# A list-scheduled two-layer decoder kernel: another order of pieces, chunks and groups, and one output store on another queue

## The chip, the cores and the metric

One core of a Trainium2 chip runs the kernel. The metric is the device time of one execution in microseconds. The kernel has one launch, and everything that it needs comes from DRAM.

## The reference

Two layers over 256 tokens of width 1024. Each layer norms x, projects it to 3584 columns that belong to three head groups, runs three kinds of attention, gates each with silu, and adds the output projection to x. A final norm follows.

```python
for layer in range(2):
    h = rms_norm(x, norm_g[layer])
    proj = einsum('btd,dc->btc', h, w_in[layer])
    sb_q, sb_k, sb_v, sb_g, mb_q, mb_k, mb_v, mb_g, mem_q, mem_g = split(proj)
    o_sb = stick_breaking(sb_q, sb_k, sb_v) * silu(sb_g)              # 6 heads of 64
    o_mb = causal softmax of rotary(mb_q), rotary(mb_k), mb_v * silu(mb_g)  # 6 heads
    m = rms_norm(mem, mem_norm_g[layer])
    mk, mv = split(einsum('bmd,dc->bmc', m, w_mem_kv[layer]))
    o_mem = softmax attention(mem_q, mk, mv) * silu(mem_g)            # 4 heads
    x = x + einsum('btc,cd->btd', concat(o_sb, o_mb, o_mem), w_out[layer])
return rms_norm(x, final_norm_g)
```

Stick-breaking weights are a sigmoid times a running product of (1 - sigmoid), worked out in log space with a cumulative sum. With 256 tokens MoBA has one block, so it is plain causal softmax.

## The kernel before

**Weights.** All weights, 81,920 words in each of 128 partitions, stream through SBUF once. They come in *pieces* (`sb_qk`, `mb_k`, `mk`, `wo0` and so on, one for each group of output columns) cut into *chunks* of some k-rows (k is one of eight blocks of 128 input rows; `NKP` says how many go into a chunk). SyncE (SP) issues a chunk's load into the ring `raw`. ScalarE (ACT) casts it to fp32r into the ring `hl` (line 287, the "hi" half), VectorE (DVE) subtracts the cast from the original (line 293, the "lo" half). TensorE (PE) then forms hi times hi, hi times lo and lo times hi. For a piece in the table `DBL` a 512-column and a 256-column matmul do this, else three 256-column ones. `HLC` is the size of the `hl` ring; the `raw` ring gets `17664 - 2 * HLC` words, so the two trade places.

**Inputs.** x comes in transposed blocks `uT`. ACT and DVE scale each by the norm's gain and split it into `T` (lines 289, 297). The row norm itself comes later: `rcx` holds it for x and `rcm` for the memory; DVE transposes it to `rt`, and it travels over DRAM to become the broadcast `rbx` or `rbm`, with which `sb_q`, `sb_k`, `mem_q` and `mem_k` are multiplied on DVE.

**Turns.** Some values have to be transposed between token and head layout. DVE transposes blocks of 32 by 32 into a buffer `D` (lines 875, 984), SP stores it to a DRAM buffer `Z` (line 1003, 128x768 words), and four or more loads bring it back turned (line 1016) to `F`, `T`, `uT` or `ga`. For a name in the table `HALVES` each of the four loads is cut into two.

**Half-array matmuls.** Scores and weighted sums of heads of 64 use 64 rows (`64*128`) or 64 columns (`128*64`) of the PE array; projections use all (`128*128`).

**Order.** Each instruction's place on its engine is fixed when the kernel is built. A list scheduler in Python holds generators (tasks) for the parts and, step by step, issues the one that can start first by planned times, broken by priorities. Its inputs are tables at the top: the order of pieces (`ORDER`), chunk sizes (`NKP`), whether a piece runs k-major (`KMAJ`), the groups of heads whose scores and weighted sums run together (`SCG`, `PVG`), priorities (`PRI`, `P_*`), the chunks behind which input blocks, x rows and constants are loaded (`X_AT`, `X0_AT`, `CST_AT`) and planned costs (`DVE_W`, `DVE_HI`, `SLACK`). On the chip each engine runs its list in order and waits on semaphores for the others.

**The end.** `out_task` ends the final norm of each of two row tiles: ACT scales columns 640 to 1023, DVE the others in two instructions, and each of the three is stored from the queue of the engine that the tuple names.

Of the kernel before, what the change touches and what calls it, by code (L numbers as in the profile page):

```python
# [41 lines left out]
PRI = ({"sb": (-170, -370), "mb": (-66, -22), "mem": (-112, 4)}, {"sb": (544, -132), "mb": (-550, -56),
       "mem": (-154, 774)})
P_EV = -3
P_H0 = -966
P_RX = -76
P_M0 = 194
P_RM = -253
P_M1 = 58
# [19 lines left out]
P_SILU = 848
SCG = (((("sb", 2), ("sb", 1)), (("sb", 0), ("mem", 1), ("mem", 0)), (("mb", 0), ("mb", 1), ("mb", 2))),  # L70
       ((("mb", 0), ("sb", 1), ("sb", 0)), (("mem", 0), ("mb", 2)), (("mb", 1),), (("sb", 2),), (("mem", 1),)))
PVG = (((("mem", 1), ("sb", 1), ("mem", 0)), (("sb", 2), ("mb", 2), ("mb", 0), ("mb", 1)), (("sb", 0),)),
       ((("mb", 0),), (("sb", 0), ("mem", 1), ("mb", 1), ("mem", 0)), (("sb", 1), ("sb", 2)), (("mb", 2),)))
# [8 lines left out]
AHEAD = 4
DVE_HI = 11539.2
SLACK_PE = 70.0
SLACK = 50.0
# [148 lines left out]
def hybrid_trunk(ctx: ExitStack, tc: tile.TileContext, x, mem, norm_g, w_in, w_mem_kv, w_out,  # L234
                 final_norm_g, xT, memT, gcols, consts, out):
    nc = tc.nc
# [762 lines left out]
    def trip(D, F, e, name, need=(), alloc=()):  # L999

        _, (Z,) = yield R("sp", alloc=["Z"])
        Zv = Z[:, :4 * e]
        nc.sync.dma_start(Zv, D[:, :4 * e])
# [8 lines left out]
        Fv = F[:, :4 * e].rearrange("p (i e) -> p i e", i=4)
        for j in range(4):
            for i0 in range(0, 4, 2 if name in HALVES else 4):
                i1 = i0 + (2 if name in HALVES else 4)
                nc.sync.dma_start(Fv[32 * j:32 * j + 32, i0:i1],
                                  Zv.rearrange("(i r) (j e) -> j r i e", i=4, j=4)[j, :, i0:i1])
# [346 lines left out]
```

## Time and profile before

| | |
|---|---|
| median of 3 runs | 268.99 us (268.93 to 269.72) |
| profiled execution, its span | 269.36 us, 267.6 us |
| PE busy | 257.0 us, 96% of the span, 1613 matmuls |
| DVE busy | 227.1 us, 85% |
| ACT busy | 193.0 us, 72% |
| SP's transfers | 77.2% of 16 DMA engines' time, 67.07 MB in all |
| granted PE clock | 0.993 of full |

The profile is of one execution. A row that groups instructions reads: line, engine, operation, output from input, shapes, count, then busy time in us and the mean of one in ns, then idle time of the engine just ahead of them and what ended it. A row of a timeline reads: start in us, duration, engine, line, operation, and in brackets the idle time before it with its releaser. `SPq` and `ACTq` rows are the engines' issuing of transfers.

### The profile page before, as it was taken

The page shows a single profiled execution, that of the slowest core. Times are in us where ns is not written, and L with a number is a line of the kernel's source. Part 1 is how long each engine was busy: PE and PEld are TensorE (multiplying, and loading weights), DVE is VectorE, ACT ScalarE, POOL GpSimd, SP SyncE. Part 2 cuts the span into 40 slices and gives each one's busy share as a digit, 9 for nine tenths or more (in the row PEclk, how much of TensorE's full clock was granted, in tenths as well). Part 3 has the DMA queues.
Part 4 walks back from the last instruction along what each step waited for, and adds up shares of the span by engine and source line. Part 5 has one row for each costly group of instructions (what it writes and reads, how often), then busy time and mean ns, then how long its engine had stood idle before and what let it go on. Part 6 is the DMA issues. An engine that isn't in the chain of part 4 may idle for free.

```text
span 267.6 us, 4996 instructions
## 1 busy us (share of the span) xinstructions
PE 257.0 (96%) x1613; PEld 228.9 (86%) x1613; DVE 227.1 (85%) x555; ACT 193.0 (72%) x429; POOL 6.2 (2%) x18
## 2 busy tenths in 40 slices
PE   8999999898999999999999999999999999999990
PEld 5878999798999997877888999888988998877880
DVE  4786988999899998999999578579999999698462
ACT  4768998689996987886876445558677988983132
POOL 1000120200000000000000000000000000000000
PEclk9999999999999999999999999999999999999997
DMA  6989999889999888997985678788597499993004
GB/s 206 367 273 342 351 393 336 289 245 277 296 305 261 263 260 284 324 299 228 299 267 178 195 182 264 221 258 275 172 283 249 162 308 282 286 281 106 0 4 157
DMA packets 50378, 67.07 MB, mean 251 GB/s; under 512 B 4720, under 2 KB 41968, under 8 KB 50352
## 3 DMA queue, kind: packets, MB, share of 16 engines
q1 hardware_dynamic: 49264, 64.65, 77.2%
q0 software_dynamic: 512, 1.31, 1.6%
q10 hardware_dynamic: 576, 0.79, 0.9%
q8 instruction: 13, 0.21, 0.3%
q14 instruction: 13, 0.11, 0.1%
HBM read 57.29 MB, written 9.44 MB: 249 GB/s over the span
## 4 chain that ended last, share of the span: by engine, by line
PE 72%; DVE 5%; DMA 5%; ACT 2%; issue 1%; ACTq 0%; DVEq 0%; SPq 0%
PE bank L270 71%; DMA gb<-in_mem_dram 3%; DMA raw<-in_w_mem_kv_dram 2%; DVE hl L293 2%; ACT junk L289 1%; DVE a L808 1%; PE bank L276 1%; DVE bank L293 1%; DVE xs L293 0%; ACT hl L287 0%; DVE gT L293 0%; DVE T L297 0%; DVE sb_k L297 0%; DVE xs L301 0%; DVE w L293 0%
## 5 line engine op out<-in xcount | busy, mean ns | idle before, releaser
L293 DVE TENSOR_TENSOR hl<-raw,hl 128x384 fp32r<-128x384 f32 (+5 forms) x146 | 103.9, 731 | 4.9 <-ACT hl L287 4.0
L270 PE MATMUL bank<-T,hl 128*128 128x256 f32 (+1 forms) x646 | 105.0, 322 | 0.7 <-DVE T L297 0.6
L287 ACT CAST hl<-raw 128x384 fp32r<-128x384 f32 (+5 forms) x144 | 91.5, 663 | 16.9 <-DMA raw<-in_w_in_dram 5.9
L270 PEld LDWEIGHTS bank<-T,hl 128*128 128x128 f32 x646 | 92.6, 189 | 11.4 <-DVE T L297 0.8
L270 PE MATMUL bank<-hl,T 128*128 128x384 f32 (+2 forms) x464 | 80.4, 330 | 0.0
L270 PEld LDWEIGHTS bank<-hl,T 128*128 128x128 f32 x464 | 77.5, 188 | 1.8 <-issue 0.7
L270 PE MATMUL bank<-hl,mxhi 128*128 128x512 f32 (+1 forms) x144 | 41.5, 369 | 0.0
L270 PEld LDWEIGHTS bank<-hl,mxhi 128*128 128x128 f32 x144 | 26.0, 188 | 5.3 <-DVE mxlo L293 0.4
L270 PE MATMUL bank<-hl,mxlo 128*128 128x512 f32 (+1 forms) x72 | 26.4, 366 | 0.0
L875 DVE STREAM_TRANSPOSE D<-w 128x384 f32<-128x384 f32 (+1 forms) x32 | 18.7, 594 | 1.0 <-ACT w L289 0.9
L289 ACT ACTIVATE junk<-xs 128x512 bf16<-128x512 f32 (+1 forms) x12 | 7.4, 613 | 16.2 <-DVE xs L293 14.7
L270 PEld LDWEIGHTS bank<-hl,mxlo 128*128 128x128 f32 x72 | 13.6, 188 | 2.2
L289 ACT ACTIVATE T<-uT,gc 128x256 fp32r<-128x256 f32 x24 | 11.6, 509 | 5.2 <-DMA uT<-xT_dram 5.0
L289 ACT ACTIVATE a<-bank 128x384 f32<-128x384 f32 x24 | 11.4, 486 | 3.7 <-DVE bank L293 2.8
L808 DVE TENSOR_TENSOR_SCAN a<-a,a 128x256 f32<-128x256 f32 (+1 forms) x24 | 12.8, 537 | 0.7 <-ACT a L289 0.7
L297 DVE SCALAR_TENSOR_TENSOR T<-uT,gc,T 128x256 fp32r<-128x256 f32 x24 | 11.3, 480 | 2.0 <-ACT T L289 1.9
L289 ACT ACTIVATE w<-w,st 128x128 f32<-128x128 f32 (+1 forms) x24 | 10.6, 444 | 0.9 <-DVE st L828 0.9
L289 ACT ACTIVATE a<-a 128x384 f32<-128x384 f32 x24 | 11.1, 520 | 0.1
L301 DVE TENSOR_SCALAR w<-w,st 128x256 f32<-128x256 f32 (+1 forms) x40 | 11.0, 323 | 0.0
L293 DVE TENSOR_TENSOR xs<-bank,xs 128x512 f32<-128x512 f32 (+1 forms) x8 | 5.3, 657 | 5.3 <-PE bank L270 5.3
L289 ACT ACTIVATE w<-bank,st 128x256 f32<-128x256 f32 x16 | 7.5, 484 | 2.1 <-DVE st L841 2.1
L828 DVE CUSTOM_DVE_ANT_0 w<-bank,cmask 128x128 f32<-128x128 f32 (+1 forms) x24 | 7.4, 347 | 1.0 <-PE bank L270 0.8
(109 smaller groups left out, 213.2 us busy)
## 6 DMA issues: line engine op xcount, KB each, us to landing
raw<-in_w_in_dram SPq DMA_DIRECT2D x28, 384.0 KB, 4.9
raw<-in_w_in_dram SPq DMA_DIRECT2D x50, 192.0 KB, 4.5
Z<-D SPq DMA_DIRECT2D x16, 384.0 KB, 4.8
raw<-in_w_out_dram SPq DMA_DIRECT2D x24, 256.0 KB, 5.5
raw<-in_w_in_dram SPq DMA_DIRECT2D x8, 576.0 KB, 5.4
raw<-in_w_mem_kv_dram SPq DMA_DIRECT2D x6, 384.0 KB, 4.5
F<-Z SPq DMA_DIRECT2D x24, 96.0 KB, 5.3
T<-Z SPq DMA_DIRECT2D x24, 96.0 KB, 4.4
```

Of the source, the lines that this page charges most:

```text
L270: nc.tensor.matmul(out, lhsT=lhsT, rhs=rhs, start=start, stop=stop, **kw)
L276: nc.tensor.transpose(out, in_, idt)
L287: nc.scalar.copy(out, in_)
L289: nc.scalar.activation(out, in_, func, **kw)
L293: nc.vector.tensor_tensor(out, a, b, op=op)
L297: nc.vector.scalar_tensor_tensor(out, a, s, b, op0=op0, op1=op1)
L301: nc.vector.tensor_scalar(out, a, s, None, op0=op)
L808: nc.vector.tensor_tensor_scan(a[:, r0:r1], a[:, r0:r1], u[:, r0:r1], 0.0, OP.add, OP.add)
L828: nc.vector.tensor_tensor_reduce(w[:, r0:r1], sc[:, r0:r1], cmask[:, 256 - r1 + r0:256], -1.0, 3.0e38, OP.add, OP.min, st[:, t:t + 1])
L875: nc.vector.transpose(o, w[:, :n * 128].rearrange("p (m j r) -> p m j r", j=4, r=32))
```

## The change

It gives new values to most tables, so the scheduler plans another order and cuts the weights into fewer, larger chunks. `HLC` goes from 6656 to 6144 words, so the `raw` ring from 4352 to 5376. Three more edits: the planned ready times of turns get 300 ns more and those of the loads of x and the memory 200 ns (in the plan only); every transfer, also one that is not issued by SP, now counts in the planner's list of transfers under way (`ring`); and the first row tile's store of columns 640 to 1023 is issued by SP instead of ACT. The names' line numbers grow by 2 or 3.

```diff
 COLS = {...}
-HLC = 6656
+HLC = 6144
 RAWC = 17664 - 2 * HLC
...
-X_AT = {7: 4, 8: 5, 11: 6, 13: 7}
-CST_AT = 34
-X0_AT = 21
+X_AT = {5: 4, 6: 5, 9: 6, 10: 7}
+CST_AT = 14
+X0_AT = 9
 X1_AT = 13
...
+ML_W = 0.0
+ML_T = 300.0
+ML_S = 200.0
 MEM_AT = 0
-ORDER = (["sb_qk", "mem_q", "mb_q", "mb_k", "mb_g", "sb_v", "mb_v", "mk", "mv", "sb_g", "mem_g"], ["mk", "mv",
-         "mb_q", "mb_k", "sb_k", "mem_q", "mb_v", "sb_q", "mem_g", "sb_v", "mb_g", "sb_g"])
+ORDER = (["sb_qk", "mb_k", "mem_q", "mb_q", "mk", "mb_v", "mv", "sb_v", "sb_g", "mb_g", "mem_g"], ["mk",
+         "mb_k", "mb_q", "mem_q", "sb_q", "sb_k", "mv", "mb_v", "mem_g", "mb_g", "sb_v", "sb_g"])
...
-HOLD = 30000.0
-HALVES = []
+HOLD = 800.0
+HALVES = [("F", 1, "sb", 2), ("F", 1, "mb", 0)]
...
 DBL = (("sb_qk", 0), ("sb_q", 1), ("sb_k", 1), ("sb_g", 1), ("mb_g", 1), ("mem_q", 0), ("mem_q", 1), ("mem_g",
-       0), ("mem_g", 1), ("mk", 1), ("mv", 1))
-DVE_W = -19195.9
+       0), ("mem_g", 1), ("mk", 1), ("mv", 0), ("mv", 1))
+DVE_W = -36995.9
...
         t = queue(_free(dst) * 4 * dst.shape[0], dst.shape[-1] * 4, now)
-        if q is None:
-            ring.append(t)
+        ring.append(t)
         if name:
-            S.ready[name] = t
+            S.ready[name] = t + {"raw": ML_W, "x": ML_S, "mem": ML_S}.get(name[0], 0.0)
...
         S.res["Z"].items.append((t, None, Z))
-        S.ready[name] = t
+        S.ready[name] = t + ML_T
         return F
...
-        for eng, a, b, q in (("act", 640, D, nc.scalar), ("dve", 0, 256, nc.sync), ("dve", 256, 640, nc.sync)):
+        for eng, a, b, q in (("act", 640, D, nc.scalar if t else nc.sync), ("dve", 0, 256, nc.sync), ("dve", 256, 640, nc.sync)):
```

The chunks change on DVE as follows: 146 subtractions (16 of 256 words, 52 of 384, 28 of 512, 34 of 768, 8 of 1024, 8 of 1152) become 107 (20 of 384, 18 of 512, 41 of 768, 14 of 1024, 6 of 1152, 8 of 1536).

First, SP's queue near the start of the program, before:

```order
L375 DMA raw<-in_w_in_dram 128x768
L375 DMA uT<-xT_dram 128x256
L375 DMA raw<-in_w_in_dram 128x768 x3
L375 DMA uT<-xT_dram 128x256
L375 DMA raw<-in_w_in_dram 128x768
L375 DMA uT<-xT_dram 128x256
L375 DMA raw<-in_w_in_dram 128x768
L375 DMA raw<-in_w_in_dram 128x256 x2
L375 DMA uT<-xT_dram 128x256
L375 DMA raw<-in_w_in_dram 128x256 x2
L375 DMA uT<-xT_dram 128x256
L375 DMA xs<-in_x_dram 128x1024
```

and now:

```order
L378 DMA raw<-in_w_in_dram 128x768
L378 DMA uT<-xT_dram 128x256
L378 DMA raw<-in_w_in_dram 128x768
L378 DMA uT<-xT_dram 128x256
L378 DMA raw<-in_w_in_dram 128x768
L378 DMA uT<-xT_dram 128x256
L378 DMA raw<-in_w_in_dram 128x768 x3
L378 DMA uT<-xT_dram 128x256
L378 DMA xs<-in_x_dram 128x1024
L378 DMA raw<-in_w_in_dram 128x384
L378 DMA uT<-xT_dram 128x256
L378 DMA raw<-in_w_in_dram 128x384 x3
```

Blocks 4 and 5 of x (the third and fourth `uT` row of the first list) stand behind earlier chunks, and the first x row tile (`xs`) comes ahead of most of them; the chunks of 256 words are gone.

Second, DVE's list just ahead of the first stick-breaking scores (`smask` rows are the work on those scores; `hl<-raw,hl` is a subtraction, `rn` and `ru` are rotary work, `ss` belongs to the memory's row norm), before:

```order
L626 TENSOR_SCALAR ss_139<-ss_139 128x1
L293 TENSOR_TENSOR ru_116<-rn_115,cst 128x6x8
L293 TENSOR_TENSOR hl<-raw,hl 128x384
L297 SCALAR_TENSOR_TENSOR mem_q<-mem_q,rbx 128x256 x2
L293 TENSOR_TENSOR rn_115<-rn_115,cst 128x6x16
L297 SCALAR_TENSOR_TENSOR sb_q<-sb_q,rbx 128x256
L293 TENSOR_TENSOR rn_115<-rn_115,ru_116 128x6x16
L297 SCALAR_TENSOR_TENSOR sb_q<-sb_q,rbx 128x256
L656 STREAM_TRANSPOSE rt<-rcm 128x32
L297 SCALAR_TENSOR_TENSOR sb_q<-sb_q,rbx 128x256
L293 TENSOR_TENSOR ru_118<-rn_117,cst 128x6x8
L297 SCALAR_TENSOR_TENSOR sb_k<-sb_k,rbx 128x256
```

and now:

```order
L300 SCALAR_TENSOR_TENSOR T_74<-uT,gc,T_74 128x256
L296 TENSOR_TENSOR hl<-raw,hl 128x768
L628 TENSOR_SCALAR ss_138<-ss_138 128x1
L296 TENSOR_TENSOR hl<-raw,hl 128x1024
L300 SCALAR_TENSOR_TENSOR mem_q<-mem_q,rbx 128x256 x2
L300 SCALAR_TENSOR_TENSOR sb_q<-sb_q,rbx 128x256 x3
L296 TENSOR_TENSOR hl<-raw,hl 128x1024
L300 SCALAR_TENSOR_TENSOR sb_k<-sb_k,rbx 128x256 x3
L296 TENSOR_TENSOR hl<-raw,hl 128x768
L296 TENSOR_TENSOR ru_116<-rn_115,cst 128x6x8
L296 TENSOR_TENSOR hl<-raw,hl 128x768
L296 TENSOR_TENSOR bank_96<-bank_96,smask 128x2x128
```

The multiplications by `rbx` now stand among two subtractions of 1024 words, without the rotary work and without the transposition of the memory's norm (`rt<-rcm`), which comes later in the list.

Third, the end of SP's queue (the last turns of layer 2 and the stores), before:

```order
L375 DMA raw<-in_w_out_dram 128x2x512 x2
L1016 DMA F_105<-Z_111 32x4x192 x4
L375 DMA raw<-in_w_out_dram 128x512 x2
L1003 DMA Z_113<-D_107 128x768
L1016 DMA T_73<-Z_112 32x4x192 x4
L375 DMA raw<-in_w_out_dram 128x512 x2
L1016 DMA F_106<-Z_113 32x4x192 x4
L1123 DMA out_dram<-xs 128x256
L1123 DMA out_dram<-xs 128x384
L1123 DMA out_dram<-xs 128x256
L1123 DMA out_dram<-xs 128x384
```

and now:

```order
L378 DMA raw<-in_w_out_dram 128x3x512
L378 DMA raw<-in_w_out_dram 128x512
L378 DMA raw<-in_w_out_dram 128x2x512 x2
L1005 DMA Z_113<-D_108 128x768
L1018 DMA T_73<-Z_112 32x2x192 x8
L1018 DMA F_105<-Z_113 32x2x192 x8
L1125 DMA out_dram<-xs 128x384
L1125 DMA out_dram<-xs 128x256
L1125 DMA out_dram<-xs 128x384
L1125 DMA out_dram<-xs 128x256
L1125 DMA out_dram<-xs 128x384
```

and the end of ACT's list, before:

```order
L289 ACTIVATE junk,ss_134<-xs 128x512
L289 ACTIVATE ss_134<-ss_134 128x1 x2
L289 ACTIVATE junk,ss_135<-xs 128x256
L289 ACTIVATE xs<-xs,ss_134 128x384
L1123 DMA out_dram<-xs 128x384
L289 ACTIVATE junk,ss_135<-bank_97 128x256
L289 ACTIVATE ss_135<-ss_135 128x1 x2
L289 ACTIVATE xs<-xs,ss_135 128x384
L1123 DMA out_dram<-xs 128x384
```

and now:

```order
L292 ACTIVATE junk,ss_135<-xs 128x256
L292 ACTIVATE xs<-xs,ss_134 128x384
L292 ACTIVATE junk,ss_135<-bank_94 128x256
L292 ACTIVATE ss_135<-ss_135 128x1 x2
L292 ACTIVATE xs<-xs,ss_135 128x384
L1125 DMA out_dram<-xs 128x384
```

Two returns of eight loads each now stand together behind the last store to `Z`, SP issues five output stores instead of four, and ACT goes from the scaling of the first row tile to the second tile's sum of squares with no transfer between. On PE there are now 11 stretches of half-array matmuls instead of 9, and 21 matmuls of 256 columns fewer ahead of the first stick-breaking scores.

More of the change, by code (lines that the diff above doesn't have):

```diff
@@ L25 @@
         "mem_q": (3072, 256), "mem_g": (3328, 256)}
-HLC = 6656
+HLC = 6144
 RAWC = 17664 - 2 * HLC
 NK = {256: 3, 384: 2, 512: 2, 768: 1}
-NKP = {("sb_q", 1): 3, ("sb_k", 0): 4, ("sb_v", 0): 1, ("sb_g", 1): 3, ("mb_q", 0): 1, ("mb_q", 1): 1, ("mb_k",
-       0): 1, ("mb_k", 1): 1, ("mb_v", 0): 3, ("mb_v", 1): 1, ("mb_g", 1): 3, ("mem_q", 0): 1, ("mem_g", 0): 1,
-       ("mem_g", 1): 4, ("mk", 0): 4, ("wo0", 0): 1, ("wo1", 0): 1, ("wo1", 1): 1}
+NKP = {("sb_k", 0): 3, ("sb_v", 1): 3, ("sb_g", 1): 4, ("mb_q", 1): 4, ("mb_k", 0): 1, ("mb_k", 1): 1, ("mb_v",
+       1): 3, ("mb_g", 1): 3, ("mem_q", 0): 2, ("mem_g", 0): 2, ("mem_g", 1): 2, ("mk", 0): 4, ("mk", 1): 4,
+       ("mv", 1): 4, ("wo0", 0): 3, ("wo0", 1): 3, ("wo1", 0): 3}
 KSPLIT = (4, 4)
-KMAJ = (("sb_q", 1), ("sb_g", 1), ("mb_v", 1), ("mb_g", 0), ("mb_g", 1), ("mem_q", 1), ("mem_g", 0), ("mk", 0),
-        ("mv", 1))
+KMAJ = (("sb_k", 1), ("sb_v", 1), ("sb_g", 0), ("mb_q", 0), ("mb_k", 0), ("mb_k", 1), ("mb_v", 0), ("mb_v", 1),
+        ("mb_g", 1), ("mem_q", 0), ("mem_q", 1), ("mem_g", 0), ("mk", 0), ("mv", 0))
 NTRIP = (0, 0)
-KORD = ((2, 3, 4, 5, 0, 1, 6, 7), (4, 5, 6, 7, 0, 1, 2, 3))
+KORD = ((2, 3, 0, 1, 4, 5, 6, 7), (4, 5, 6, 7, 0, 1, 2, 3))
 LAT_SAME, LAT_CROSS = 130.0, 240.0
@@ L41 @@
 COLD = 3900.0
[L42 to L49, printed above, removed]
+PRI = ({"sb": (-1494, -1070), "mb": (-780, -100), "mem": (-1672, -146)}, {"sb": (-38, -6), "mb": (-1502,
+       -1898), "mem": (-184, 522)})
+P_EV = -1047
+P_H0 = 28
+P_RX = -442
+P_M0 = -424
+P_RM = 1289
+P_M1 = -280
 URG = 2
-X_AT = {7: 4, 8: 5, 11: 6, 13: 7}
-CST_AT = 34
-X0_AT = 21
+X_AT = {5: 4, 6: 5, 9: 6, 10: 7}
+CST_AT = 14
+X0_AT = 9
 X1_AT = 13
@@ L68 @@
 TABLE = 1290.0
[L69 to L73, printed above, removed]
-HOLD = 30000.0
-HALVES = []
-CROWD = 45
-SPARE1 = 0
-SPARE2 = 0
-DBL = (("sb_qk", 0), ("sb_q", 1), ("sb_k", 1), ("sb_g", 1), ("mb_g", 1), ("mem_q", 0), ("mem_q", 1), ("mem_g",
-       0), ("mem_g", 1), ("mk", 1), ("mv", 1))
-DVE_W = -19195.9
[L82 to L85, printed above, removed]
+P_SILU = -378
+SCG = (((("mb", 1), ("mb", 2), ("sb", 1)), (("mem", 0), ("mem", 1)), (("mb", 0),), (("sb", 2),), (("sb", 0),)),
+       ((("mb", 0), ("sb", 1)), (("sb", 0), ("sb", 2)), (("mb", 2),), (("mem", 0), ("mem", 1)), (("mb", 1),)))
+PVG = (((("mb", 1), ("sb", 1), ("sb", 0)), (("mb", 0), ("sb", 2)), (("mem", 0), ("mb", 2)), (("mem", 1),)),
+       ((("mb", 1), ("mb", 2), ("sb", 0), ("mem", 1), ("mem", 0), ("sb", 1)), (("mb", 0), ("sb", 2))))
+HOLD = 800.0
+HALVES = [("F", 1, "sb", 2), ("F", 1, "mb", 0)]
+CROWD = 2
+SPARE1 = 4
+SPARE2 = 1
+DBL = (("sb_qk", 0), ("sb_q", 1), ("sb_k", 1), ("sb_g", 1), ("mb_g", 1), ("mem_q", 0), ("mem_q", 1), ("mem_g",
+       0), ("mem_g", 1), ("mk", 1), ("mv", 0), ("mv", 1))
+DVE_W = -36995.9
+AHEAD = 181
+DVE_HI = 17839.2
+SLACK_PE = 60.0
+SLACK = 0.0
 def _free(ap):
```

## The prediction

> **What bounds the kernel now.** I read the page's engine totals and chain first, then the windows by stage, the waits of TensorE (PE), the groups by shape, and last the timelines at the places where something ends late.
>
> ```profile
> PE 257.0 (96%) x1613; PEld 228.9 (86%) x1613; DVE 227.1 (85%) x555; ACT 193.0 (72%) x429; POOL 6.2 (2%) x18
> PE 72%; DVE 5%; DMA 5%; ACT 2%; issue 1%; ACTq 0%; DVEq 0%; SPq 0%
> 0.00:45.00 45.00, 43.06 (x242) 38.06 (x243) 34.73 (x80) 34.67 (x83) 3.44 (x13) 1.00 0.95 325
> 45.00:135.00 90.00, 87.98 (x601) 78.83 (x600) 86.47 (x226) 74.64 (x166) 2.25 (x4) 1.00 0.91 279
> 135.00:245.00 110.00, 110.00 (x668) 98.33 (x666) 94.89 (x223) 78.41 (x165) 0.54 (x1) 1.00 0.79 238
> ...
> PE bank L270 <- DVE sb_k L297: 1.3, 1, 1.3
> PE bank L270 <- DVE junk L1129: 1.2, 1, 1.2
> PE bank L270 <- DMA raw<-in_w_mem_kv_dram: 0.7, 1, 0.7
> PE bank L270 <- DVE T L297: 0.6, 1, 0.6
> ```
>
> The windows give, after the stretch and its length, the busy time of PE, weight load, DVE, ACT and POOL, then the granted clock, the DMA share and GB/s. PE carries the end: it is idle 1.94 us in the first 45, 2.02 in the next 90 and not at all from 135 to 245. The waits name nearly all of that: 1.2 at the very start, which no order moves, and 1.3, 0.7 and 0.6, together 2.6 us. So a new order can win 2.6 us plus what it finds in the last 10 us. It can lose more, because DVE is busy 86.47 of 90 us from 45 to 135: whatever it does late there, PE feels. Before 45 us DVE idles 10.27.
>
> The profiled execution took 269.36 us, 1.8 more than its span of 267.6; the median of the runs is 268.99, 0.37 lower. 0.3% of it, 0.8 us, is about what a measurement tells from no change.
>
> **The change part by part.** *Fewer, larger weight pieces.* Each piece costs an ACT cast and a DVE subtraction.
>
> ```profile
> L293 DVE TENSOR_TENSOR hl<-raw,hl 128x768 fp32r<-128x768 f32 x34 | 31.6, 945 | 2.2 <-ACT hl L287 2.0
> L293 DVE TENSOR_TENSOR hl<-raw,hl 128x384 fp32r<-128x384 f32 x52 | 27.4, 549 | 0.9 <-ACT hl L287 0.5 <-DMA raw<-in_w_in_dram 0.2
> L293 DVE TENSOR_TENSOR hl<-raw,hl 128x512 fp32r<-128x512 f32 x28 | 18.6, 680 | 0.0
> L293 DVE TENSOR_TENSOR hl<-raw,hl 128x1152 fp32r<-128x1152 f32 x8 | 10.7, 1336 | 0.7 <-ACT hl L287 0.6
> L293 DVE TENSOR_TENSOR hl<-raw,hl 128x1024 fp32r<-128x1024 f32 x8 | 9.7, 1209 | 0.0
> L293 DVE TENSOR_TENSOR hl<-raw,hl 128x256 fp32r<-128x256 f32 x16 | 6.3, 416 | 1.1 <-ACT hl L287 0.9
> L297 DVE SCALAR_TENSOR_TENSOR T<-uT,gc,T 128x256 fp32r<-128x256 f32 x24 | 11.3, 480 | 2.0 <-ACT T L289 1.9
> ```
>
> Busy over count gives 0.39 us for 256 words, 0.53 for 384, 0.66 for 512, 0.93 for 768, 1.21 for 1024, 1.34 for 1152; by the step from 768 to 1152 I estimate 1.75 for 1536. The 146 subtractions (104.3 us) become 107: 20 of 384, 18 of 512, 41 of 768, 14 of 1024, 6 of 1152 and 8 of 1536, or 10.6 + 11.9 + 38.1 + 16.9 + 8.0 + 14.0 = 99.5. That is 4.8 off DVE; some copies of values that move to DVE (about six at 0.3) take back 1.8. Net 3 us less DVE work, none of it on PE's path by itself; it counts where PE waits for DVE.
>
> *The first wait, 0.6 at 14.5.* PE waits there for the fifth or so piece of T, the scaled input. The new order loads input pieces 4 and 5 behind weight chunks 5 and 6 instead of 7 and 8, and the raw ring holds 1024 words more. SP issues a load in about 0.45 us (below), so the piece leaves SP about 0.9 us earlier, more than the 0.6. I take −0.6; 0 if ACT, which makes half of T, is late for its casts instead.
>
> *The second wait, 1.3 at 49.7.* The first stick-breaking scores wait for sb_k times rbx on DVE.
>
> ```profile
> 40.01 0.56 DVE L293 TENSOR_TENSOR ru<-rn,cst 128x48 f32<-128x48 f32 x4
> ...
> 45.68 0.15 DVE L626 TENSOR_SCALAR ss<-ss 128x1 f32<-128x1 f32 x1 [0.79 <-ACT junk L289]
> 48.24 0.20 DVE L656 STREAM_TRANSPOSE rt<-rcm 128x32 f32<-128x32 f32 x1
> 49.24 0.41 DVE L297 SCALAR_TENSOR_TENSOR sb_k<-sb_k,rbx 128x256 f32<-128x256 f32 x1
> ...
> 49.71 1.58 PE L270 MATMUL bank<-sb_k,sb_q 64*128 64x128 f32 x16 [1.27 <-DVE sb_k L297]
> 51.22 6.01 PE L270 MATMUL bank<-T,hl 128*128 128x256 f32 x48
> ```
>
> In the new order 21 fewer 256-column matmuls stand ahead of these scores: at 6.01/48 = 0.125 us PE arrives 2.6 us earlier. Ahead of the last sb_k piece DVE has nine subtractions of 384 and eight of 256 less (−4.7, −3.1), four of 512 and two of 1024 more (+2.7, +2.4), two more pieces of T (+0.9), and four ru, three rn, an rt and an ss less (four ru took 0.56 together; nine at that rate are −1.2): −3.0. So DVE gains 0.4 on PE by work alone. Of its idle time the 0.79 before ss stands in this stretch; in the new order that row norm of the memory comes later, and the norm of x, which rbx holds, is transposed right behind the first sb_q piece. If that idle goes, the wait is about gone; if DVE idles as before, 0.9 is left. I take −0.6, with ends 0 and −1.3.
>
> *The third wait, 0.7 at 66.3* (the first scores on turned q and k). In the new layer 0 mb_k is projected second and mb_q fourth, with mk behind, where before both were followed at once by mb_g. The k turn then has over 10 us to spare by my count, the q turn none or 2 us. I take −0.5, ends 0 and −0.7.
>
> *mv of layer 0 doubled*: 16 groups of three 256-column matmuls become one of 512 and one of 256.
>
> ```profile
> 190.09 11.30 PE L270 MATMUL bank<-T,hl 128*128 128x512 f32 x64
> 244.79 0.28 PE L270 MATMUL bank<-hl,mxhi 128*128 128x256 f32 x1
> 245.00 0.87 PE L270 MATMUL bank<-T,mb_v 128*64 128x256 f32 x8
> ...
> 247.10 0.39 PE L270 MATMUL bank<-hl,mxhi 128*128 128x256 f32 x1
> 247.33 0.28 PE L270 MATMUL bank<-hl,mxlo 128*128 128x256 f32 x1
> 247.44 0.40 PE L270 MATMUL bank<-hl,mxhi 128*128 128x256 f32 x2
> ```
>
> The row at 190.09 alternates the two widths (11.30/64 = 0.177 each), so a group costs 0.353 instead of 3 × 0.125: −0.35 in all, and 0 where DVE holds PE anyway. I take −0.3.
>
> *More changes between whole-array and half-array matmuls.* The new order has 11 stretches of half-array work (64 rows or columns) instead of 9. Between starts a 256-column matmul takes 0.11 us (247.33 to 247.44); entering such a stretch takes 0.21 (244.79 to 245.00) and leaving it 0.23 (247.10 to 247.33): some 0.2 more a stretch, +0.4 for two. The end near nothing is 0, where PE waits anyhow, the other 0.8 if the drain is twice that in the long matmuls.
>
> The Trainium skill, "TensorEngine Tiling (Array Packing)", section "Key Properties", says that changing the tiling mode drains TensorE. It gives no figure; the 0.2 us above bears it out, and by the page alone the sum would be what it is with the +0.4, without it 0.4 lower.
>
> *The last turns of layer 2.* HALVES cuts two returns from four loads to eight. They stand last in SP's queue, 16 issues where eight stood, and one of them is the one that ends last.
>
> ```profile
> 234.01 0.33 SPq L1003 DMA_DIRECT2D Z<-D  x1
> 240.38 1.80 SPq L1016 DMA_DIRECT2D F<-Z  x4
> ...
> Z<-D SPq DMA_DIRECT2D x3, 384.0 KB, 5.9
> F<-Z SPq DMA_DIRECT2D x12, 96.0 KB, 5.6
> T<-Z SPq DMA_DIRECT2D x4, 96.0 KB, 3.9
> ```
>
> Issues cost 1.80/4 = 0.45 us. Before, the last return is issued by 242.18 and takes 3.9 to 5.6 to land (medians from issue to landing), and PE uses it from 245.7: hardly any slack. Eight more issues are 3.6 us, of which the two weight loads that stood between them (now ahead of the last Z store) give back 0.9, and the T return can be issued while the last Z store is under way. A return of half the size should land sooner. DVE transposes the last w about 2 us of its own work later in the order, less the 3 us that it saves. Between 0 (all hidden) and +3.6 (no cover), I take +0.5, near the lower end, since most of the issues overlap the store's 5.9 us.
>
> *The store moved from ACT to SP.*
>
> ```profile
> 260.65 0.61 ACT L289 ACTIVATE xs<-xs,ss 128x384 f32<-128x384 f32 x1
> 261.30 0.35 ACTq L1123 DMA_DIRECT2D out_dram<-xs  x1
> 261.44 2.91 SPq L1123 DMA_DIRECT2D out_dram<-xs  x4
> 261.70 0.38 ACT L289 ACTIVATE junk<-bank 128x256 bf16<-128x256 f32 x1 [0.43 <-ACT xs L289]
> 263.41 0.39 ACTq L1123 DMA_DIRECT2D out_dram<-xs  x1
> ```
>
> ACT's last sum of squares waits 0.43 us behind its own store issue, and the whole end of the second row tile hangs on it. Without the issue: −0.4. SP issues five stores instead of four, but its first is ready at 261.3 and its fourth and fifth only near 263, so the extra 0.45 falls into time when SP has nothing to do. Ends: −0.45, and 0 if a store of the first tile holds back one of the second.
>
> The Trainium skill, "DMA: Bandwidth & Descriptors", section "Issuing engines are not separate DMA queues", says that issuing from several engines saves only sequencer time, usually small beside the DMA. By that rule the move is worth nothing and the sum would be 0.4 higher; here the sequencer time sits on the chain (0.43 us of waiting at 261.70), so the row decides.
>
> *What I cost at nothing*: the order of the gates' activations, the ready times added to loads (they only move planned order), the constants and x's first row tile loaded earlier: 0.92 MB, at the window's 325 GB/s 2.8 us by which weights come later for a while. The raw ring's extra 1024 words in 128 partitions, 0.52 MB, cover 1.6 of it and DVE's idle time before 45 the rest; without that cover it would be 1.2 more of rival three's kind.
>
> Sum: −0.6 − 0.6 − 0.5 − 0.3 + 0.4 + 0.5 − 0.4 = −1.5. From 269.36 that is 267.9, from the median 267.5; I give **267.7 us**, with an own range of 266.8 to 268.3.
>
> **The rivals.** *One, nothing won.* DVE's 10.27 us of idle before 45 stays, PE arrives just as late behind it, and only −0.4 at the tail, −0.3 for mv and +0.4 for the switches are left, with the start's 0.6 perhaps: 268.4 to 269.4. For it: DVE is 96% busy to 135, so a gain ahead is paid back there. Against: 3 us less DVE work.
>
> *Two, slower by the last turns.* The 16 return issues run one after the other behind the last Z store and PE stands still before its last 81 matmuls. Price up to 3.6; with the rest of the sum (−2.0) that gives 270.6 to 271. It decides from a wait of 2.8 up, where the whole comes out over 0.8 slower. For it: no slack there before. Against: the T return's issues fit beside the store.
>
> *Three, slower by large pieces.* A matmul can't start before its whole piece is loaded, cast and subtracted; two 1024-word pieces (1.21 us DVE each) now stand right among sb_q, sb_k and rbx, and 1152- and 1536-word pieces fill layer 2. If PE waits about 1.2 twice and the memory's norm, transposed some 20 us later than its 48.24, is late for the memory scores by 1 to 2, the whole is 270 to 271.
>
> *Four, all waits go.* −0.6 − 1.3 − 0.7 − 0.3 + 0.4 − 0.4, nothing at the last turns: 266.1 to 266.5.
>
> **How the numbers follow.** My forecast has 0.40, rival one 0.25, two 0.12, three 0.10, four 0.13. Faster by over 0.8 us: the forecast and four, 0.53. Within: rival one, 0.25. Slower: two and three, 0.22. The range of 8 in 10 goes from the middle of rival four, 266.0, to 270.2, which leaves out the upper two thirds of rivals two and three (0.15) and the lowest part of four (0.04).
>
> **What would show it.** Right: DVE subtractions near 99.5 us in 107; no wait for T near 14; a wait under 0.8 before the first sb scores, near 47; PE busy within 1 us of 256; no wait before the last half-array stretch over 1 us; ACT's last sum of squares right behind xs with no store between. Wrong: a PE wait of over 1 us at a place that has none in the list above, most likely for F or T near 243 or for DVE between 60 and 130; or DVE idle before 45 above 10 us with the wait at sb_k unchanged.

## The result, and the profile after

The changed kernel takes 266.16 us (median of 4 runs, 265.58 to 266.48), the kernel before 269.36 beside it: a ratio of 0.9869, with a 95% interval of 0.9825 to 0.9913. A second group on another chip gave 0.9878 (0.9826 to 0.9930). So 3.2 us are gone by these medians and 3.3 to 3.5 by the ratios, more than twice the 1.3 of the forecast (267.7 against 268.99). The time lies below the forecast's own range (266.8 to 268.3), inside the range of 8 in 10 at its low end (266.0), and in that of rival four. A few executions came out over 1.5% slower than the fastest of their kernel and are left out of every ratio.

The page of the changed kernel (engine totals, chain, the largest group), its waits of PE and its windows by stage:

```profile
PE 256.1 (97%) x1597; PEld 227.6 (86%) x1597; DVE 225.0 (85%) x517; ACT 190.2 (72%) x393; POOL 6.1 (2%) x18
PE 87%; DMA 7%; ACT 1%; SPq 1%; DVE 1%; issue 0%; DVEq 0%; ACTq 0%
L296 DVE TENSOR_TENSOR hl<-raw,hl 128x768 fp32r<-128x768 f32 (+5 forms) x107 | 99.6, 947 | 7.9 <-ACT hl L290 6.0
...
PE bank L273 <- DVE junk L1131: 1.2, 1, 1.2
PE bank L273 <- DMA T<-Z: 0.3, 1, 0.3
PE bank L273 <- DVE T L300: 0.2, 1, 0.2
...
0.00:45.00 45.00, 43.57 (x249) 38.61 (x249) 36.39 (x81) 34.89 (x75) 3.30 (x13) 1.00 0.97 333
45.00:135.00 90.00, 89.75 (x599) 79.96 (x599) 85.43 (x208) 74.48 (x160) 2.26 (x4) 1.00 0.93 287
135.00:245.00 110.00, 110.00 (x682) 97.82 (x681) 95.89 (x213) 75.70 (x143) 0.55 (x1) 1.00 0.74 229
```

The profiled execution took 265.58 us, its span is 263.8; the one of the kernel before took 269.36, with a span of 267.6, so the profiles lie 3.8 us apart, somewhat more than the medians. Of the three waits (1.3, 0.7 and 0.6 us) none is left; two small ones have come, 0.3 and 0.2. PE loses 0.25 us of the 90 from 45 to 135, where it lost 2.02. The subtractions are 107 in 99.6 us, as worked out (99.5); DVE as a whole is busy for 2.1 us less, where 3 were worked out. Against the kernel before the span is 3.8 us shorter: 2.3 of idle PE time, 0.85 of PE's busy time (257.0 to 256.1) and the rest behind PE's last matmul, which ended at 260.93 before and now:

```profile
257.53 0.28 PE L273 MATMUL bank<-hl,mxhi 128*128 128x256 f32 x1
...
257.52 0.62 ACT L292 ACTIVATE xs<-xs,ss 128x384 f32<-128x384 f32 x1
258.05 0.36 ACT L292 ACTIVATE junk<-bank 128x256 bf16<-128x256 f32 x1
258.17 2.50 SPq L1125 DMA_DIRECT2D out_dram<-xs  x5
259.74 0.37 ACTq L1125 DMA_DIRECT2D out_dram<-xs  x1
```

That is 257.81, so the tail went from 6.65 to 5.99 us. The last sum of squares (`junk`) starts 0.53 us behind the start of `xs`, where it was 1.05.

### The profile page after: what moved, and what is told of

Same layout as the page of the kernel before. It is cut to its first block, busy times and chain, and to the rows that moved or that the text cites. A ratio compares the mean times of both kernels' runs of the same rounds, so it can differ in the third digit from the quotient of the medians.

```text
span 263.8 us, 4793 instructions
## 1 busy us (share of the span) xinstructions
PE 256.1 (97%) x1597; PEld 227.6 (86%) x1597; DVE 225.0 (85%) x517; ACT 190.2 (72%) x393; POOL 6.1 (2%) x18
## 4 chain that ended last, share of the span: by engine, by line
PE 87%; DMA 7%; ACT 1%; SPq 1%; DVE 1%; issue 0%; DVEq 0%; ACTq 0%
PE bank L273 86%; DMA T<-Z 3%; DMA raw<-in_w_out_dram 3%; DMA raw<-in_w_in_dram 2%; PE bank L279 1%; SPq L1018 1%; ACT hl L290 1%; ACT junk L292 1%; DVE xs L296 1%; SPq L378 0%; DVE xs L304 0%; ACT ss L292 0%; DVE T L300 0%; DVEq L1362 0%; DVE ss L628 0%
## 5 line engine op out<-in xcount | busy, mean ns | idle before, releaser
L296 DVE TENSOR_TENSOR hl<-raw,hl 128x768 fp32r<-128x768 f32 (+5 forms) x107 | 99.6, 947 | 7.9 <-ACT hl L290 6.0
L273 PE MATMUL bank<-T,hl 128*128 128x256 f32 (+1 forms) x646 | 106.1, 322 | 0.2 <-DVE T L300 0.2
L290 ACT CAST hl<-raw 128x768 fp32r<-128x768 f32 (+5 forms) x105 | 85.3, 841 | 17.0 <-DMA raw<-in_w_in_dram 6.4
L273 PE MATMUL bank<-hl,T 128*128 128x384 f32 (+1 forms) x448 | 79.6, 335 | 0.0
L273 PEld LDWEIGHTS bank<-hl,T 128*128 128x128 f32 x448 | 76.5, 188 | 2.2 <-issue 0.3
L292 ACT ACTIVATE w<-w,st 128x128 f32<-128x128 f32 (+1 forms) x24 | 10.7, 448 | 2.3 <-DVE st L830 2.2
L292 ACT ACTIVATE a<-a 128x384 f32<-128x384 f32 x24 | 11.8, 522 | 0.2
L304 DVE TENSOR_SCALAR w<-w,st 128x256 f32<-128x256 f32 (+1 forms) x40 | 11.2, 323 | 0.2
L290 ACT COPY gT<-bank 128x256 f32<-128x256 f32 x10 | 3.6, 372 | 7.7 <-PE bank L273 7.7
```

Of the source, the lines that this page charges most:

```text
L273: nc.tensor.matmul(out, lhsT=lhsT, rhs=rhs, start=start, stop=stop, **kw)
L290: nc.scalar.copy(out, in_)
L292: nc.scalar.activation(out, in_, func, **kw)
L296: nc.vector.tensor_tensor(out, a, b, op=op)
L304: nc.vector.tensor_scalar(out, a, s, None, op0=op)
```

## The experiments

Where an order is "held", the sequence of steps that the planner chose for the named kernel is recorded and replayed, so that only the edit shown differs; the others were planned anew. The one-line store edits move only that store. Ratios are to the kernel before on the same chip; the unchanged copies of the changed kernel stand at 0.9869 and 0.9878.

### A yardstick, and the tail

`after_again`, the changed kernel unedited:

> The changed kernel once more, beside the kernel before on one chip, as the yardstick of this group. Theory A (its gain is the three PE waits that are gone, 2.3 us, PE's own stream 0.8 us shorter and the tail 0.7 us shorter, all set by the order): 3.2 to 3.9 us below the kernel before, with the same two small waits (about 0.25 us each, near 7 and 115 us). Rival B (the first comparison caught slow executions of the kernel before): 2.2 us or less below it.

0.9878 (0.9826 to 0.9930), 265.67 us. Theory A. In this execution PE has no wait at all but that for its start:

```profile
PE bank L273 <- DVE junk L1131: 1.2, 1, 1.2
```

On the two small waits near 7 and 115 us theory A was wrong: they are not the order's own but come and go with the execution. The times vary by more than the smaller terms of the sum: the kernel before lay between 267.68 and 271.05 us beside this group, the changed kernel between 265.19 and 268.1.

`tail_store_back`:

```diff
-nc.scalar if t else nc.sync
+nc.scalar
```

> The changed kernel with the first row tile's store of columns 640 to 1023 issued by ACT again; every other list is unchanged. Theory A (ACT's own issue stands on the chain to the end): the last sum of squares starts 0.4 to 0.5 us later behind xs and the time is 0.4 to 0.5 us above the changed kernel. Rival B (the tail's 0.7 us come from SP's queue or from the landing of the stores): under 0.2 us, and the gap behind xs does not matter.

Ratio 0.9893 (0.9843 to 0.9942), 266.17 us: 0.5 above the yardstick, which these times alone can't resolve. Its end on ACT:

```profile
257.45 0.62 ACT L292 ACTIVATE xs<-xs,ss 128x384 f32<-128x384 f32 x1
258.09 0.35 ACTq L1125 DMA_DIRECT2D out_dram<-xs  x1
258.49 0.38 ACT L292 ACTIVATE junk<-bank 128x256 bf16<-128x256 f32 x1 [0.43 <-ACT xs L292]
```

The last sum of squares again starts 1.04 us behind xs. Both executions have no PE wait, and the spans are 263.8 and 264.3. Theory A: the issue was on the chain, and a transfer's issue of 0.35 us cost 0.5. The time from PE's last matmul to the end bears it out in every profile without extra traffic: 6.0 to 6.1 us with the store on SP, 6.6 to 6.7 with it on ACT, in both orders.

`before_sp_store`, the same one line on the kernel before:

> The kernel before with only the first row tile's store of columns 640 to 1023 moved from ACT's to SP's queue; all other lists unchanged. Theory A (ACT's issue is on the chain to the end, as the 0.55 us of the opposite edit on the changed kernel says): 0.4 to 0.6 us below the kernel before, ACT's last sum of squares within 0.1 us of the end of xs. Rival B (a fifth issue on SP holds the last store back in this order): within 0.2 us of it.

Ratio 1.0004 (0.9969 to 1.0040): not resolved by the times. The spread of this kernel, over 3 us, hides half a microsecond. The tail itself is as theory A has it: PE's last matmul ends at 261.12 of a span of 267.2, 6.1 us ahead of the end instead of 6.65. The waits of PE say why the time shows nothing:

```profile
PE bank L270 <- DVE hl L293: 1.3, 2, 1.0
PE bank L270 <- DVE junk L1129: 1.2, 1, 1.2
PE bank L270 <- DVE T L297: 0.5, 1, 0.5
PE bank L270 <- DVE sb_k L297: 0.4, 1, 0.4
```

Up to the last microseconds this is the kernel before, instruction for instruction, yet sb_k costs 0.4 instead of 1.3, the turned q and k have no wait in the list, and 1.3 us are lost to the subtractions instead. The list of waits on which the forecast rests was one draw, and so is any wait that one profile of an edit shows.

### Do single edits carry over to the old order?

`before_early_loads` (order held):

```diff
-X_AT = {7: 4, 8: 5, 11: 6, 13: 7}
-CST_AT = 34
-X0_AT = 21
+X_AT = {5: 4, 6: 5, 9: 6, 10: 7}
+CST_AT = 14
+X0_AT = 9
```

> The kernel before with the order of all engines' work held, and only the input blocks, the first x row tile and the constants loaded behind the earlier chunks of the changed kernel (5, 6, 9, 10; 9; 14). Theory A (the wait for T at 14.5 us is a late load, and the sb_k wait is what DVE idles for before): the 0.6 us at 14.5 goes and the sb_k wait changes by less than 0.4; 0.3 to 0.9 us below the kernel before. Rival B (the short raw ring makes it worse, because weights are displaced by 0.92 MB and this ring has no room to make up): the sb_k wait grows, and the total is 0 to 2 us above the kernel before.

1.0038 (1.0003 to 1.0073). Rival B by its total, which is not faster, but not by its mechanism: the sb_k wait did not grow, it was 0.5 in the profiled execution, between the 1.3 and 0.4 without the edit. The wait for T near 14.5 was 0.3, so it did not go.

`before_mem_norm_later` (seven steps of the memory's norm moved in the held order):

```diff
-ACT sum, DVE ss, ACT sum, ACT Ln, ACT Exp, DVE rt<-rcm, POOL rows   (among mem_q, sb_q, sb_k times rbx)
+the same seven behind the last sb_k<-sb_k,rbx
```

> The kernel before with the order held, except that the second half of the memory's row norm (ACT's two sums, its root, DVE's ss and the transposition rt) is moved behind the multiplications of sb_k by rbx on ACT and DVE. Theory A (the sb_k wait at 49.7 us is DVE idle time behind ACT, which waits 1.2 us for the load of the memory rows): DVE's 0.8 us of idle near 45.7 goes and the PE wait for sb_k falls from 1.3 to 0.3 to 0.6 us; the total is 0.5 to 1 us below the kernel before if nothing later takes it back. Rival B (the idle only moves, since the casts behind it wait for loads anyway): the wait stays at 1.1 us or more.

```profile
PE bank L270 <- DMA raw<-in_w_mem_kv_dram: 1.6, 1, 1.6
PE bank L270 <- DVE junk L1129: 1.2, 1, 1.2
PE bank L270 <- DVE T L297: 0.8, 1, 0.8
PE bank L270 <- DVE sb_k L297: 0.6, 1, 0.6
```

The sb_k wait is 0.6 here, as theory A had it, and the next one, at 66.6 us, is 1.6. But without the edit sb_k was 1.3 in one execution and 0.4 in another, so the profile does not show that the edit moved either wait. The total does decide: 1.0063 (1.0030 to 1.0095), slower and not faster. That the wait was handed on fits this and is not shown.

`before_three_edits` (both, and the SP store):

> The three edits together on the kernel before's order: SP store, earlier loads, memory norm later. Theory A (each removes its own wait): about 1.5 to 2.2 us below the kernel before, about half of the change's gain without its new order. Rival B (a wait that goes is taken back at the next tight place, since DVE is busy 96% of 45 to 135 us): only the tail's 0.5 us and at most 0.3 more.

1.0047 (1.0017 to 1.0076). Neither theory: it is slower. Its profile has no wait for sb_k, but 1.1 us at 66 (put down to the turned q and k, `uT<-Z`) and 0.9 for T, although the input blocks are loaded as early as in the changed kernel. Edits at single waits of the old order gain nothing.

### Where the spare time is

`split_subtract` (order of the changed kernel held):

```diff
-            tt(los(j), raws(j), his(j).bitcast(F32), OP.subtract)
+            n = hlp[j][2]
+            for a, b in ((0, n // 2), (n // 2, n)) if n >= 512 and j < 40 else ((0, n),):
+                tt(los(j)[:, a:b], raws(j)[:, a:b], his(j)[:, a:b].bitcast(F32), OP.subtract)
```

> The changed kernel, same order, but each of the first 40 pieces of 512 words or more is subtracted on DVE in two halves instead of one instruction (loads and casts as they are), which costs DVE about 0.13 us a piece, as small pieces do. 16 of these stand ahead of the first stick-breaking scores, so 2.1 us more DVE work there. Theory A (larger pieces are what takes the sb_k wait away): a PE wait of 0.8 to 1.6 us for sb_k near 45 us, 1 to 2.5 us above the changed kernel. Rival B (DVE has idle time to spare ahead of the scores, the piece count does not matter): no PE wait over 0.4 there and less than 0.5 us in all.

0.9874 (0.9830 to 0.9918), 266.1 us. Rival B. The sb_k rows on DVE and PE's row behind them, of the changed kernel and of this one:

```profile
43.03 1.09 DVE L300 SCALAR_TENSOR_TENSOR sb_k<-sb_k,rbx 128x256 f32<-128x256 f32 x3
44.94 1.58 PE L273 MATMUL bank<-sb_k,sb_q 64*128 64x128 f32 x16
...
44.45 1.09 DVE L300 SCALAR_TENSOR_TENSOR sb_k<-sb_k,rbx 128x256 f32<-128x256 f32 x3
44.92 1.60 PE L273 MATMUL bank<-sb_k,sb_q 64*128 64x128 f32 x16
```

The three `sb_k` pieces of a row are ready one by one, 0.33 us apart. PE starts on the first (44.87): here at 44.92 us, while the last is ready at 45.54. In the old order it started on the second (49.65, PE at 49.71, the third not before 49.75). So in the changed kernel's profile PE arrives 1.5 us behind the piece that it needs (43.45), where the old one had a wait of 1.3. This reserve wanders as the waits do: it is 0.6 in after_again, and in whole_returns, which is the same program up to there, PE waits 0.3. For the same reason the shift of 1.42 us between the two rows can't be put down to the edit: in after_again, unedited, the row starts at 44.12. What the run shows is its time, with no loss from 2.1 us of DVE work: the number of pieces on DVE alone is not what removed the wait.

`before_extra_traffic` and `after_extra_traffic` (each in its own order, held; `late` is a buffer in DRAM that nobody reads):

```diff
+        at = sum(len(c[1]) * c[3] for c in chunks[:j])
+        for n in range(4):
+            if at < 4096 * (n + 1) <= at + len(kk) * w:
+                nc.sync.dma_start(late[:, n, :], w_out[1].rearrange("(k p) c -> p k c", p=128)[:, n, 0:512])
```

> The kernel before with the order held and four more transfers that nobody reads, 256 KB each from one DRAM place to another, issued by SP between the weight loads of layer 0 (about every 4096 words of weights), so that the loads behind them come later. The four take about 1 MB / 325 GB/s = 3.2 us of the DMA engines. Theory A (the kernel before has no spare, each late load reaches PE; the changed order has some): 2 to 5 us above the kernel before. Rival B (both orders lose alike): the same loss as the changed kernel with the same transfers, within 0.7 us.

> The changed kernel with the order held and the same four transfers at the same places of the weight stream. Theory A (the changed order holds spare time, 1.4 us ahead of the first scores, and a deeper raw ring): 0 to 1.5 us above the changed kernel, at least 1.5 less than the kernel before loses. Rival B (both are bound by the stream of weights in layer 0): 2 to 5 us above it.

The kernel before goes to 1.0133 (1.0081 to 1.0185), 3.6 us up. The changed kernel stands at 0.9883 (0.9836 to 0.9930), 266.39 us, 0.2 to 0.7 above its own medians. Theory A, in both. The waits of the kernel before under this traffic, and its windows around the first (busy time of PE first, the granted clock third from the end), and PE's first row behind it:

```profile
PE bank L270 <- DVE sb_k L297: 3.7, 1, 3.7
PE bank L270 <- DVE junk L1134: 1.2, 1, 1.2
...
48.00:52.00 4.00, 0.31 (x3) 0.11 (x1) 4.00 (x17) 4.00 (x12) 1.50 (x3) 0.84 0.85 283
52.00:54.00 2.00, 1.99 (x14) 1.81 (x16) 2.00 (x7) 0.55 (x2) 0.18 (x1) 0.50 0.97 353
54.00:56.00 2.00, 2.00 (x11) 1.35 (x10) 2.00 (x7) 1.13 (x3) 0.00 (x0) 0.50 0.74 258
56.00:58.00 2.00, 2.00 (x13) 2.00 (x13) 2.00 (x6) 2.00 (x6) 0.57 (x1) 0.61 0.94 221
...
52.02 2.93 PE L270 MATMUL bank<-sb_k,sb_q 64*128 64x128 f32 x16 [3.70 <-DVE sb_k L297]
```

and of the changed kernel:

```profile
PE bank L273 <- DVE sb_k L300: 1.4, 1, 1.4
PE bank L273 <- DVE junk L1136: 1.2, 1, 1.2
PE bank L273 <- DMA T<-Z: 0.4, 1, 0.4
...
48.00:52.00 4.00, 4.00 (x35) 3.94 (x34) 4.00 (x13) 2.86 (x7) 0.00 (x0) 1.00 1.03 305
```

The same 1 MB makes a wait of 1.4 us here and of 3.7 there. It delays the piece of sb_k that PE needs by 2.3 us in the old order's profile (49.65 to 51.96) and by 3.0 in the new one's (43.45 to 46.48), so not by less; the changed order had a reserve in front of it, the old one a wait already. The rest of the difference is the granted clock, which fell behind the long wait: the span of the old order's profile is 4.8 us longer than without the traffic, of which 1.8 are waits and 2.8 slower matmuls. Each profile is one execution; that of the changed kernel (267.45 us) is one of the two slowest of its six.

`short_raw_ring` and `ring_512_less` (order held; only the load ring is shorter):

```diff
-RAWC = 17664 - 2 * HLC
+RAWC = 17664 - 2 * HLC - 1024      (ring_512_less: - 512)
```

> The changed kernel with the order of all engines' work held as it is, and only the raw ring cut from 5376 to the 4352 words of the kernel before, so weight loads are issued later. Theory A (the waits are gone because DVE has less and better placed work ahead of PE, not because weights lie ready earlier): 0 to 0.5 us above the changed kernel, no PE wait over 0.5. Rival B (the deeper ring is what took the waits away): ACT's casts wait longer for loads, PE waits return before 70 us, 1 to 2.5 us above the changed kernel.

> The changed kernel with the order held and the raw ring cut by half as much as in the run with 4352 words: 4864 words. Theory A (the spare time is the ring's depth, word by word): the loss is about half of that run's, 5 to 10 us. Rival B (a threshold: the ring must only hold the largest pieces that follow each other, and 4864 words do): under 1.5 us above the changed kernel.

1.0524 (1.0472 to 1.0576), 283.86 us, and 1.0194 (1.0146 to 1.0241), 274.27 us: 18.2 and 8.6 us above the yardstick (the second ran on another chip; its ratio gives 8.5). Rival B in the first, and far beyond its numbers; theory A in the second. PE's waits with 4352 words, and ACT's casts in the yardstick and here (idle time before them last):

```profile
PE bank L273 <- DVE mxhi L311: 4.7, 1, 4.7
PE bank L273 <- ACT uT L290: 2.0, 2, 1.7
PE bank L273 <- DVE sb_k L300: 1.8, 1, 1.8
...
L290 ACT CAST hl<-raw 128x768 fp32r<-128x768 f32 (+5 forms) x105 | 85.3, 839 | 16.9 <-DMA raw<-in_w_in_dram 5.1 <-DMA raw<-in_w_out_dram 4.4 <-PE bank L273 3.5
L290 ACT CAST hl<-raw 128x768 fp32r<-128x768 f32 (+5 forms) x105 | 86.1, 842 | 42.3 <-DMA raw<-in_w_in_dram 21.8 <-DMA raw<-in_w_out_dram 10.3 <-PE bank L273 6.2
```

The casts' wait for loads goes from 9.5 to 32.1 us. Both runs keep an order that was planned for 5376 words, so they price the ring for this order and not for the best one with a shorter ring. That large pieces make depth worth more, since a load needs a large hole in the ring, is likely but no run here shows it.

`old_tables_new_ring`, `HLC = 6144` alone in the kernel before, and `raw_ring_deeper`, `HLC = 5888` in the changed one; both planned anew:

> The kernel before with HLC = 6144 alone, so a raw ring of 5376 words and 512 words less for the split weights; the planner orders anew with the old tables. Theory A (the ring alone is the spare): 2 to 4 us below the kernel before, and its executions lie within 3 us of each other. Rival B (the smaller hl ring and an order whose tables were not chosen for it cost more than the depth brings): 0 to 4 us above the kernel before.

> The changed kernel's tables with HLC = 5888, so a raw ring of 5888 words instead of 5376; the planner orders anew. Theory A (PE has no waits left, more spare brings nothing, and a smaller hl ring makes PE's releases stand in the way): 0 to 3 us above the changed kernel. Rival B (more depth, more spare): 0.3 to 1 us below it, executions closer together.

1.0200 (1.0149 to 1.0250), 274.95 us, and 1.0549 (1.0508 to 1.0591), 284.12 us. The ring alone is not the spare time, and more of it, taken from the `hl` ring, is worse. Both keep their tables and get an order that these were not chosen for, so what the smaller `hl` ring costs by itself stays open.

### The small terms

`whole_returns` (order held):

```diff
-HALVES = [("F", 1, "sb", 2), ("F", 1, "mb", 0)]
+HALVES = []
```

> The changed kernel with the order held and the two last turns of layer 2 returned in four loads each instead of eight. Theory A (the last turns have slack in this order, halving is worth nothing): within 0.3 us of the changed kernel, no PE wait over 0.2 after 220 us in either. Rival B (the halves land sooner and that is what keeps PE from waiting): a PE wait of 0.3 to 1.5 us near 242 and that much more time. Rival C (eight more issues cost, as the prediction's +0.5 has it): up to 0.5 us below the changed kernel.

0.9865 (0.9820 to 0.9911), 265.85 us. Theory A: no difference. The rows of the changed kernel show the slack that the forecast missed (SP's issues, what the F returns take from issue to landing, PE's use of them):

```profile
228.88 6.62 SPq L1018 DMA_DIRECT2D T<-Z  x8
235.61 4.07 SPq L1018 DMA_DIRECT2D F<-Z  x8
F<-Z SPq DMA_DIRECT2D x8, 48.0 KB, 1.9
...
243.22 0.82 PE L273 MATMUL bank<-F,sb_v 128*64 128x256 f32 x8
```

The last issue ends at 239.68; at 1.9 us to landing it is in place at about 241.6, 1.6 ahead of PE. Whole returns of 96 KB land in 2.4 us in this order. In the kernel before, the last return by itself took this from issue to landing:

```profile
DMA to landing us min/median/max: 2.8/3.1/3.3
```

That is less than the 3.9 to 5.6 us of the prediction, which are medians over all returns of that stretch to F, most of them earlier, and over the one to T.

`mv_not_doubled`:

```diff
-("mk", 1), ("mv", 0), ("mv", 1))
+("mk", 1), ("mv", 1))
```

> The changed kernel with mv of layer 0 out of the table DBL (the planner moves a few rows on PE and DVE). 16 groups of 512 and 256 columns become three of 256 each. Theory A (the row of the trace: 0.51 us less PE time): 0.4 to 0.6 us above the changed kernel. Rival B (the saving is taken back by the two DVE additions that it needs): within 0.2 us.

0.9848 (0.9808 to 0.9888), 265.8 us, so by the times not dearer. By the spans of two executions without any PE wait, 264.3 against the yardstick's 263.8, it is 0.5. The times can't settle it; the rows are with theory A.

`extra_half_switches` (order held):

```diff
+        if first and p.name[:2] == "wo":
+            mm(acc[:, 0:128], a[:64], hi[:64, o:o + 128], True, True)
```

> The changed kernel with the order held and eight more matmuls of 64 rows by 128 columns (they write what the next matmul overwrites), one ahead of each accumulation of the output projections; six of them make a half-array stretch of their own. Theory A (a stretch costs 0.2 us beside its matmuls, as the prediction has it): 8 matmuls of about 0.06 us and 6 stretches, 1.5 to 1.9 us above the changed kernel. Rival B (it costs 0.4, both drains in full): 2.6 to 3.2 us. Rival C (the drain hides behind waits for DVE): under 0.8 us.

1.0015 (0.9978 to 1.0053), 269.27 us, 3.6 above the yardstick in median and 3.0 in span. No PE wait is in this execution, so the span is the better measure: 3.0 less eight matmuls of 0.06 leaves 2.5. In the trace seven of the eight, not six, stand alone among whole-array matmuls (the eighth, at 118.15 us, follows a stretch of 64 columns), so about 0.36 for each. Rival B. PE's timeline at one of them (two matmuls in the first row, the extra and the next real one):

```profile
106.03 0.75 PE L273 MATMUL bank<-hl,mxhi 64*128 64x128 f32 x2
106.61 0.39 PE L273 MATMUL bank<-hl,mxlo 128*128 128x512 f32 x1
106.84 0.62 PE L273 MATMUL bank<-hl,mxhi 128*128 128x512 f32 x2
```

From 106.03 to 106.61 are 0.58 us for an extra matmul and a 512-column one that takes 0.23 (106.61 to 106.84). No run adds whole-array matmuls instead, so the price of the change is not separated from that of the extra matmul's own weight load.

## Why the prediction was wrong in size

The direction and the tail held; the sum came out at under half. By the profiles the span fell by 3.8 us where −1.5 was summed. The steps that failed, in us: the waits (−1.7 summed, −2.3 measured), PE's own stream of matmuls (+0.1, from −0.3 for mv and +0.4 for the stretches; −0.85 measured), the last turns (+0.5; 0) and the tail (−0.4; −0.66). Point by point:

- **What bounds it: held, but read as fixed.** "A new order can win 2.6 us plus what it finds in the last 10 us" took the waits of one execution for the kernel's own. They wander (before_sp_store), and edits at single waits of the old order gain nothing (before_mem_norm_later, before_three_edits). What the changed kernel has is spare time: the same extra 1 MB costs 3.6 us before and 0.2 to 0.7 after. This is shown, with the lower clock behind the long wait as part of the 3.6. That this order needs the ring's depth, 8.6 us for the first 512 words and 9.6 for the next, is shown too; how much of the spare comes from `ORDER`, the chunk sizes or the places of the loads one by one is not.
- **The first wait: −0.6 forecast, 0.6 gone, but not by the cause named alone.** The forecast gave it to the earlier input blocks and the longer ring. With the earlier blocks in the old order the wait for T was 0.3 and 0.9 (before_early_loads, before_three_edits), so they alone do not remove it. What did stays open.
- **The second wait: −0.6 forecast, 1.3 gone.** Two things were missed. The work was counted up to the last piece of sb_k, where PE waits for the second before and the first now. And the idle time was halved as unknown: up to the piece that PE needs DVE is busy for 34.84 us instead of 38.56 and idle for 8.6 instead of 11.1 (9.6 in after_again), while PE arrives 3.5 earlier. The work thus keeps pace with PE, and the idle time, which wanders, makes the reserve.
- **The third wait: −0.5 forecast, 0.7 gone.** Nothing speaks against the mechanism; the size was cut for doubt. The profile names a weight load at this wait, in before_three_edits the turned q and k.
- **The last turns of layer 2: +0.5 forecast, 0 measured.** The step that failed is the landing time: 3.9 to 5.6 us from medians, where the last return itself took 3.1. In the new order the weights are loaded by then and the halves land in 1.9, whole returns in 2.4.
- **The tail: −0.4 forecast, −0.66 in the profiles, of which 0.5 is the store.** The mechanism was right: the sequencer time was on the chain. The Trainium skill, "DMA: Bandwidth & Descriptors", section "Issuing engines are not separate DMA queues", says that several issuing engines save only sequencer time, usually small beside the DMA; here that time was 0.35 us on ACT and 0.5 of the kernel. What the other 0.1 is stays open.
- **mv: −0.3 forecast, −0.5 by span.** Right in sign, unresolved in the times.
- **Half-array stretches: +0.4 forecast, +0.7 by the price measured.** Two stretches at 0.36. The step that failed took entry and exit as one row's excess each; the matmul behind each change is late as well. The Trainium skill, "TensorEngine Tiling (Array Packing)", section "Key Properties", has the drain without a figure; the run gives it one.
- **A term put at nothing: how close matmuls follow each other inside the score stretches.** With the terms above the span would be about 1 us longer than it is. Summed from start to start, with the listed waits left out, PE's matmuls inside these stretches take 10.7 us in the changed kernel's profile where they took 11.5; no term of the forecast has this. In after_again it is 10.7 again, but 11.2 in split_subtract and 11.5 in whole_returns; the profiles of the old order without extra traffic have 11.2 to 11.8, so part of it may be waits too short to be listed. Why they are closer was not tested.
- **The range.** 266.0 is called the middle of rival four, which is 266.1 to 266.5, so it lies below all of that rival. With the true middle, 266.3, the range of 8 in 10 would have missed 266.16.

Rival four had the mechanism (all waits go) and the time, 266.1 to 266.5, at a chance of 0.13. That its time fits is in part luck: its sum of −2.9 has PE's own stream at +0.1 as well, and it meets a gain of 3.2 by the medians where the profiles, from which its terms are read, lie 3.8 apart. Rivals two and three did not occur; PE waits behind late loads where the ring was cut, but large pieces were not tested by themselves.

## What to carry to other kernels

Read the waits of several executions before taking them for terms of a sum: where two engines run neck and neck, the waits of one profile are a sample, and removing one need not shorten the whole. A test with some extra traffic, in the old and in the new order, tells whether an order has spare time; here it separated them by 3 us while edits at single waits gained nothing. Ring depth and order belong together: the new ring with the old tables cost 5 us, the new order with a load ring as short as the old one 18, and both together gained 3.

## What the hardware showed

A wait of 3.7 us on PE cost more than itself: the granted clock stood at 0.50 to 0.61 from 52 to 58 us in before_extra_traffic, and PE's matmuls from 52.0 to 54.9 took 2.9 us, where the same 16 took 1.58 in the changed kernel. After waits of 1.4 us (after_extra_traffic, 1.00 throughout 48 to 52) and 2.2 us (ring_512_less, its longest) nothing of that kind is seen. The Trainium skill, "TensorE: Matmul & The Clock Gate", section "What's actually happening", puts the fall to half clock at an idle window of about 3.4 us; the waits of 3.7, 1.4 and 2.2 us agree with it.

In old_tables_new_ring the clock fell without any such wait. PE's rows and the window behind them (granted clock third from the end):

```profile
108.91 0.47 PE L270 MATMUL bank<-hl,mxhi 128*128 128x512 f32 x1 [1.68 <-ACT hl L287]
109.74 0.50 PE L270 MATMUL bank<-hl,mxlo 128*128 128x512 f32 x1 [0.36 <-DVE mxlo L293]
110.08 0.40 PE L270 MATMUL bank<-hl,mxhi 128*128 128x512 f32 x1
110.70 0.58 PE L270 MATMUL bank<-hl,mxhi 128*128 128x512 f32 x1 [0.22 <-DVE mxhi L308]
...
111.00:114.00 3.00, 3.00 (x8) 2.24 (x8) 3.00 (x8) 2.97 (x5) 0.00 (x0) 0.50 0.89 300
```

Three waits of 1.68, 0.36 and 0.22 us within 3.5 us came before it, and no others within 5 us. That is less than the idle window which the page names, so here the run decides: it is not the longest wait alone that counts. For a planner it means that a delay is cheap up to some point and then costs nearly twice: in before_extra_traffic 3.7 us of waiting and 2.8 of slower matmuls. That is one more reason for spare time ahead of PE.
